# A hybrid decoder layer on one core: the first FFN block scaled between the last residual additions, the FFN zone's tags in another order, and all low parts of the first activations on VectorE

## The chip, the cores and the metric

The kernel runs on one core of one Trainium2 chip. The metric is the device time of one execution in microseconds, the median of several runs. TensorE (PE) multiplies matrices, with its weight loads (PEld) beside them; VectorE (DVE), ScalarE (ACT) and GpSimd (POOL) work element by element; SyncE (SP) holds the queue from which the transfers between HBM and the on-chip memory (SBUF) are issued, in order. Each engine runs its own instructions in a fixed order and waits on semaphores for the others. TensorE adds up in PSUM, eight banks that DVE and ACT empty.

## The reference, cut to what matters

One layer of a decoder on a prompt of 1,024 positions and 8 sequences of 8 new positions, 1,088 columns in all. Model width is 1,024, FFN width 2,816.

```
h = rms_norm(x, norm_mix_g);  proj = h @ w_in
a = silu(layer_norm(conv31(a_val * sigmoid(a_gate))))
o = attend(q, k, v)                       # three dilated windows merged
x = x + concat([a, o]) @ w_out            # residual, then:
h = rms_norm(x, norm_ffn_g)
g = conv3(concat([ffn_past, h @ w_ffn_gate]))
x = x + (silu(g) * (h @ w_ffn_up)) @ w_ffn_down
y = rms_norm(x, norm_final_g)
```

The change lies from the end of `@ w_out` to the start of `@ w_ffn_down`.

## The kernel before, in words

**Number format.** A float32 operand is split into a high part (`hi`, ACT's copy to a rounded type) and a low part (`lo = x - hi`, a subtraction on DVE or POOL). A product takes three matmuls: weights hi by x hi, hi by lo, lo by hi. Lines 908, 910, 911 (`block_product`), 926, 928, 930 (`two_products`) and 182 to 184 (`gemm`) are such triples.

**Zones.** SBUF is handed out in zones that follow each other. Zone F holds the end of the output projection and the FFN; zone D, the down projection, comes after it in the same place; zones G and U (parts of the output projection, masks and caches of the attention on new positions) and P (masks, queries, keys, values of the attention on the prompt) lie under F. A zone's tags lie one behind the other in the order in which each is first asked for, and a tile waits only for the readers of what lay in its own bytes before (`reuse_waits="tile"`). So the order of first requests sets which early reader each tile waits for. Before, F's order is b11, t2, b21, WA, t4, t1, t3, tmp, b22, sft, cfo. Most are tags of 8 slots of 544 columns (`slot`, L896); WA has 2 of 1,024 columns, tmp 4 of 544; sft and cfo hold the FFN convolution's states. Within a tag the first request takes the lowest slot, the next ones come from the top downwards. That puts t2 and the first slot of b21 on the operands of zone G, which the products of the second part of the output projection read to their end. In zone D the 24 slots of tag X (1,088 columns, the first activations' hi and lo) start at the same address as F: the first tile on F's lowest tag, the other eleven of the first group at the top of X, on t3, t1, t4 and the end of WA.

**End of the output projection (L942 to L1079).** The last two of eight input tiles are loaded in halves of 544 columns (L949), split (L951 on ACT, L952 on DVE), and so are their weights (L962, L963). `out_half(h, hook)` runs over the eight output tiles m of one half: a product of 12 matmuls, the residual addition on DVE (L1045), a store of x, the square on ACT (L1048) and its addition to a running sum on DVE (L1052). `hook` is called at the end of each m. In the second half it puts in the norm of the first half: `root` after m = 2 (10 small matmuls at L204, small DVE operations L206 to L219, a square root on ACT), `spread` after m = 5 (5 transposes L231, copies L233), which gives the scale `rb` per column.

**First blocks of the FFN (L1072 to L1136).** The FFN products work on 2 by 2 blocks in the manner of Winograd and Strassen: seven block products from seven tags b11 ... t4. `first_blocks` scales four tiles of x (`scale`, L1058 on DVE) and splits each (`split`, L972 on ACT, L973 on DVE) into b11, then b21. Its orders: the scaling waits for the last but one split, or, ahead of the first two, for `after`, the last addition of squares; each split waits for `after` too. `first_half` starts the gate's products on b11 with `two_products`. The second half's norm follows the same way.

**FFN pairs (L1175 to L1250).** Eleven pairs of tiles: gate products, convolution, up products, and `u = silu(g) * up` (L1217 is its multiplication, L1226 the additions ahead of it), which is stored to HBM. Each set of products reads the blocks in the order b11, t2, b21, t1, t3, b22, t4. `weight_blocks` makes seven weight blocks by additions on DVE and splits on ACT (L1001) and POOL (L1002).

**Down projection (L1264 to L1330).** u is read back in groups of 3 + 3, 3 + 3, 3 + 3 and 2 + 2 tiles: load (L1268, SP queue), high part on ACT (L1269), low part (L1271) on DVE, or on POOL for numbers 3 and 5 of all (`ONPOOL`). For each output tile m, weights are split (L156 on ACT, L158 on POOL), and chunks of 384, 384 and 320 columns are multiplied and added to x on DVE (L1301). x is read back from HBM by `reload`; the last two tiles of u are stored at m = 0 (L1295). PSUM has five banks for these products, so the sixth chunk needs the first to be empty. `behind(late, early)` orders two instructions of one engine; `AHEAD` puts some low parts ahead of the last pair's operations: number 1 ahead of the last addition to u, number 4 ahead of the last two multiplications.

The order of instructions on every engine is made at build time by a scheduler that runs its own model of the program; `tc.issue_after` and `behind` are orders given to it by hand.

Of the kernel before, what the change touches and what calls it, by code (L numbers as in the profile page):

```python
# [60 lines left out]
AHEAD, ONPOOL = ((1, 2), (4, 0), (4, 1)), (3, 5)  # L61
# [17 lines left out]
def trunk_kernel(tc, xT, w_in, w_out, w_gate, w_up, w_down, par, kc, vc, sa, sf, pmask, smask,  # L79
                 yT, kT, vT, ca, cas, cf):  # L80
    nc = tc.nc
    with (
# [60 lines left out]
        def behind(late, early):  # L143

            tc.add_manual_dep(late, early.name, mybir.DependencyInfo(mybir.DependencyClass.NoSync,
                                                                     mybir.DependencyReason.DATA))
# [794 lines left out]

        k0 = first[0]  # L942
        n = PARTS[-1]
        part = []
        for h, tag in enumerate(("b11", "t2")):
            part.append([])
            for i in range(n):
                raw = slot("b11", "mx", F32)
                last_load = nc.sync.dma_start(raw, mixed[k0 + i][:, h * HN:h * HN + HN]).ins  # L949
                hi, lo = slot(tag, "mh"), slot(tag, "ml")  # L950
                nc.scalar.activation(hi, raw, AF.Copy)  # L951
                nc.vector.tensor_sub(lo, raw, hi.bitcast(F32))  # L952
                part[h].append((hi, lo))
        wl = []
        for m0 in (0, 4):
# [3 lines left out]
            for i in range(2):  # L959
                r = raw[:, i * 512:i * 512 + 512]  # L960
                hi, lo = slot("b21", "wh", w=512), slot("b21", "wl", w=512)
# [35 lines left out]
        def block_tile(x, zone=False):  # L997

            t = zt("F", "WA", 2, "wa", D, F32R) if zone else wp.tile([P, D], F32R, tag="W", name=nm("wb"))
# [8 lines left out]
        def weight_blocks(w, j):  # L1008
# [6 lines left out]
            nc.vector.tensor_add(x, u1, u2)  # L1015
# [14 lines left out]
        for i in range(2):  # L1030
            up0 += weight_parts(raw[0][:, i * half:i * half + half], [slot("t4", "wa", w=half) for _ in range(2)])
# [5 lines left out]
        def out_half(h, hook):  # L1037


            c = slice(h * HN, h * HN + HN)  # L1040
            for m in range(KT):
# [3 lines left out]
                added = nc.vector.tensor_add(x, all_of(ps), x).ins  # L1045
# [3 lines left out]
                if m == 0:  # L1049
                    acc = s  # L1050
                else:
                    added = nc.vector.tensor_add(acc, s, acc).ins  # L1052
                hook(m, added)
            return acc, added
# [5 lines left out]
        def new_root(s):  # L1060
            return slot("t3", s, F32)

        sq0, _ = out_half(0, lambda *_: None)
        rs = []

        def norm_first(m, added):
            if m == 2:
                rs.append(root(sq0, D, HN))
            elif m == 5:
                rs[0] = spread(rs[0], new_root, HN)  # L1070

        def first_blocks(k, tag, after):  # L1072
            for i in range(k, k + 4):
                with tc.issue_after(made[-2] if len(made) > 1 else after):
                    scale(0, i, rs[0])
                with tc.issue_after(after):
                    split(x2[i][:, :HN], tag, i - k)

        sq1, added = out_half(1, norm_first)  # L1079
        quads = [(*halves(x2[k]), *halves(x2[k + 4])) for k in range(4)]  # L1080

        def first_half(w, between=lambda: None, hook=lambda k, last: None):
# [4 lines left out]
            shared = [zt("F", "tmp", 4, "ta", HN) for _ in o]  # L1087
# [16 lines left out]
        def between():  # L1104
            rs.append(root(sq1, D, HN))
            first_blocks(4, "b21", added)
# [6 lines left out]
        first_blocks(0, "b11", added)  # L1113
# [24 lines left out]
        sft = zt("F", "sft", 1, "sft", NF * B * 2).rearrange("p (j b t) -> p j b t", b=B, t=2)  # L1138
        nc.sync.dma_start(sft, sf)
        cfo = zt("F", "cfo", 1, "cfo", NF * 18).rearrange("p (j c) -> p j c", c=18)  # L1140
# [24 lines left out]
        stores, timed = [], {}  # L1165
# [9 lines left out]
        def ffn_pair(j):  # L1175
# [40 lines left out]
            def times(i, a, e):  # L1216
                timed[i] = nc.vector.tensor_mul(u[i][:, a:min(e, S)], u[i][:, a:min(e, S)], cv[i][:, a:min(e, S)]).ins  # L1217
# [44 lines left out]
        split_last = []  # L1262

        def load_act(j):  # L1264
# [5 lines left out]
            eng = nc.gpsimd if len(split_last) in ONPOOL else nc.vector  # L1270
            split_last.append(eng.tensor_sub(lo, raw, hi.bitcast(F32)).ins)  # L1271
# [14 lines left out]
        def down(j0, n, act, first, between):  # L1286
            for m in range(KT):
# [12 lines left out]
                def ev(ps, t0, n, x=x2[m]):  # L1300
                    nc.vector.tensor_add(x[:, t0:t0 + n], ps[:, :n], x[:, t0:t0 + n])  # L1301
# [22 lines left out]
        for k, i in AHEAD:  # L1324
            behind(timed[i], split_last[k])
# [171 lines left out]
```

## Time and profile before

| | us |
|---|---|
| runs | 1393.05, 1383.58, 1389.17; median 1389.17 |
| profiled execution | 1384.67 (span 1382.3, mean granted clock 0.991) |
| TensorE busy, matmul / weight loads | 1340.1 / 1274.5 |
| DVE, ACT, POOL busy | 832.9, 522.7, 429.3 |

The stages around the change: the second part of the output projection ends near 586 us from the span's start, its last part ends near 622, the FFN's products run to 1099, and the down projection starts there.

How to read the lines: a timeline row is start, duration, engine, source line, operation, output <- inputs, sizes, and how many instructions were merged (xN); in brackets stand the idle time of the engine before it and what ended it. A row of waits is who waited, for whom, total time, how often, the longest. A row of a group is the line, engine, operation, count, then minimum/median/maximum duration in ns. "Half clock" is a granted TensorE clock of 0.50.

### The profile page before, as it was taken

How to read it: one execution, taken by the hardware profiler on the slowest of the kernel's cores; microseconds unless marked ns; L12 is line 12 of the kernel's file. 1: busy time of each engine (PE TensorE's matmuls, PEld its weight loads, DVE VectorE, ACT ScalarE, POOL GpSimd, SP SyncE). 2: the span in 40 equal slices, each digit the busy share in tenths (PEclk: the TensorE clock that was granted, in tenths of full speed). 3: DMA queues.
4: the chain of work that ended last, by engine and by line, in shares of the span. 5: the costliest groups of instructions: out<-in, count | busy, mean ns of one | idle time of the engine just before them, and what ended most of it. 6: DMA issues, size and time to landing. Idle time of an engine off the chain costs nothing.

```text
span 1382.3 us, 25035 instructions
## 1 busy us (share of the span) xinstructions
PE 1340.1 (97%) x10059; PEld 1274.5 (92%) x10059; DVE 832.9 (60%) x1660; ACT 522.7 (38%) x1047; POOL 429.3 (31%) x341
## 2 busy tenths in 40 slices
PE   7999999999999999998999999999999999999996
PEld 7998888989978877888999999999999989999996
DVE  6478878566585566578865655665656661313156
ACT  6322221457575465255533333333333430202122
POOL 1221112111010103430865554555644332223200
PEclk9999999999999999989999999999999999999998
DMA  8247675746688976460111222202212481314103
GB/s 281 68 152 274 234 264 183 204 132 154 210 269 247 268 215 229 135 206 16 64 57 68 95 79 79 94 32 95 94 64 94 140 303 54 136 46 144 40 18 113
DMA packets 85747, 195.16 MB, mean 141 GB/s; under 512 B 12672, under 2 KB 47744, under 8 KB 85632
## 3 DMA queue, kind: packets, MB, share of 16 engines
q1 hardware_dynamic: 85632, 193.57, 43.6%
q8 instruction: 79, 1.29, 0.4%
q14 instruction: 36, 0.29, 0.1%
HBM read 145.03 MB, written 48.52 MB: 140 GB/s over the span
## 4 chain that ended last, share of the span: by engine, by line
PE 88%; DMA 6%; DVE 4%; issue 1%; ACT 1%; SPq 0%; POOL 0%; DVEq 0%; ACTq 0%; POOLq 0%
PE g L182 12%; PE g L184 12%; PE g L183 12%; PE py L910 4%; PE py L908 4%; PE py L911 4%; PE o L734 3%; PE pz L910 3%; PE pz L911 3%; PE pz L908 3%; PE px L910 3%; PE px L911 3%; PE px L908 3%; PE s L649 3%; PE t L717 2%; PE ss L568 1%
## 5 line engine op out<-in xcount | busy, mean ns | idle before, releaser
L158 POOL TENSOR_TENSOR wl<-wr,wh 128x768 fp32r<-128x768 f32 (+2 forms) x60 | 114.5, 1910 | 484.9 <-PE g L184 390.7
L182 PE MATMUL g<-xh,wh 128*128 128x384 f32 (+1 forms) x472 | 158.1, 335 | 0.6 <-DVE qkv L445 0.6
L183 PE MATMUL g<-xl,wh 128*128 128x384 f32 (+1 forms) x472 | 156.9, 332 | 0.0
L184 PE MATMUL g<-xh,wl 128*128 128x384 f32 (+1 forms) x472 | 156.7, 332 | 0.0
L182 PE MATMUL g<-ah,wh 128*128 128x384 f32 (+1 forms) x432 | 140.1, 328 | 3.0 <-DVE x L1301 3.0
L184 PE MATMUL g<-ah,wl 128*128 128x384 f32 (+1 forms) x432 | 140.9, 327 | 1.7 <-POOL wl L158 1.7
L183 PE MATMUL g<-al,wh 128*128 128x384 f32 (+1 forms) x432 | 141.4, 328 | 0.4 <-POOL al L1271 0.3
L1002 POOL TENSOR_TENSOR wb<-wr,wb 128x512 fp32r<-128x512 f32 x84 | 115.6, 1388 | 56.5 <-ACT wb L1001 56.5
L156 ACT ACTIVATE wh<-wr 128x768 fp32r<-128x768 f32 (+2 forms) x60 | 50.0, 833 | 218.9 <-PE g L184 170.9
L1001 ACT ACTIVATE wb<-wr 128x512 fp32r<-128x512 f32 x84 | 52.6, 629 | 163.7 <-DVE wr L1017 104.0
L1301 DVE TENSOR_TENSOR x<-g,x 128x384 f32<-128x384 f32 (+1 forms) x72 | 37.9, 533 | 123.3 <-PE g L184 123.3
L690 ACT ACTIVATE y<-y,m 128x128 f32<-128x128 f32 (+1 forms) x192 | 88.9, 466 | 19.6 <-DVE m L678 19.5
L182 PEld LDWEIGHTS g<-xh,wh 128*128 128x128 f32 x472 | 89.2, 189 | 2.9 <-issue 1.6
L184 PEld LDWEIGHTS g<-xh,wl 128*128 128x128 f32 x472 | 89.2, 189 | 2.3 <-issue 2.1
L1207 DVE SCALAR_TENSOR_TENSOR fc<-gb,prm,fc 128x1104 f32<-128x1104 f32 x44 | 81.8, 1877 | 14.8 <-ACT fc L1205 14.5
L183 PEld LDWEIGHTS g<-xl,wh 128*128 128x128 f32 x472 | 89.4, 189 | 0.6 <-issue 0.2
L653 DVE CUSTOM_DVE_ANT_0 y<-s,pmk 128x128 f32<-128x128 f32 (+1 forms) x192 | 64.1, 379 | 41.7 <-PE s L649 31.9
L1002 POOL TENSOR_TENSOR wa<-wr,wa 128x512 fp32r<-128x512 f32 x42 | 56.0, 1336 | 100.9 <-ACT wa L1001 100.9
L395 DVE SCALAR_TENSOR_TENSOR cacc<-gp,prm,cacc 128x1024 f32<-128x1024 f32 x60 | 86.7, 1444 | 0.0
L182 PEld LDWEIGHTS g<-ah,wh 128*128 128x128 f32 x432 | 81.0, 188 | 3.8 <-DVE x L1301 3.5
L184 PEld LDWEIGHTS g<-ah,wl 128*128 128x128 f32 x432 | 81.1, 188 | 2.0 <-POOL wl L158 2.0
L183 PEld LDWEIGHTS g<-al,wh 128*128 128x128 f32 x432 | 81.2, 188 | 1.0 <-POOL al L1271 0.6
(359 smaller groups left out, 4091.0 us busy)
## 6 DMA issues: line engine op xcount, KB each, us to landing
cr<-in_kc SPq DMA_DIRECT2D x24, 768.0 KB, 6.8
cr<-in_vc SPq DMA_DIRECT2D x24, 768.0 KB, 7.4
kk<-dk SPq DMA_DIRECT2D x48, 256.0 KB, 5.9
u<-u SPq DMA_DIRECT2D x22, 544.0 KB, 4.7
al<-u SPq DMA_DIRECT2D x22, 544.0 KB, 5.1
wr<-in_w_gate SPq DMA_DIRECT2D x22, 512.0 KB, 3.4
wr<-in_w_up SPq DMA_DIRECT2D x22, 512.0 KB, 4.6
wr<-in_w_in SPq DMA_DIRECT2D x20, 512.0 KB, 5.5
```

What stands on the lines that cost most here:

```text
L158: lo_eng.tensor_sub(lo, raw, hi.bitcast(F32))
L182: nc.tensor.matmul(ps[c], whi[:, k, :], xh[:, t0:t0 + n], start=(k == 0), stop=False)
L183: nc.tensor.matmul(ps[c], whi[:, k, :], xl[:, t0:t0 + n], start=False, stop=False)
L184: nc.tensor.matmul(ps[c], wlo[:, k, :], xh[:, t0:t0 + n], start=False, stop=(k == nk - 1))
L395: eng.scalar_tensor_tensor(acc[:, :S], gp[:, j:j + S], col(w0 + j), acc[:, :S], op0=ALU.mult, op1=ALU.add)
L653: nc.vector.tensor_tensor_reduce(out=y[:, o:o + n], in0=ps[:, o:o + n], in1=mask, op0=ALU.add, op1=ALU.min, scale=1.0, scalar=3e38, accum_ ...
L690: nc.scalar.activation(y, y, AF.Exp, bias=m[:, 4 * g + i:4 * g + i + 1], scale=-1.0, accum_out=den[:, g, 2 * hd + u, i:i + 1])
L908: nc.tensor.matmul(ps, whi[:, k, :], xh[:, t], start=(start and k == 0), stop=False, skip_group_check=True)
L910: nc.tensor.matmul(ps, whi[:, k, :], xl[:, t], start=False, stop=False, skip_group_check=True)
L911: nc.tensor.matmul(ps, wlo[:, k, :], xh[:, t], start=False, stop=(k == nk - 1), skip_group_check=True)
L1002: nc.gpsimd.tensor_sub(lo, x, hi.bitcast(F32))
L1207: nc.vector.scalar_tensor_tensor(c[:, :W], gb[i][:, t:t + W], col(C_FW + 3 * f + t), c[:, :W], op0=ALU.mult, op1=ALU.add)
```

## The change

It does four things.

1. `norm_first` is called for the root after m = 3 and for the spread after m = 6, one product later each.
2. `first_blocks` gives up `after`: the first two scalings wait for the residual additions of products 6 and 7 of the second half, no longer for the last addition of squares, and the splits wait for nothing by hand. `out_half` returns its residual additions. The first addition of `weight_blocks` is put behind the last split of b21 (`made[7]`).
3. The tags of zone F are asked for in another order, by a block of early requests: cfo, sft, WA, tmp, t4, t3, b21, t2, b11, then t1, b22. The tiles asked for early are handed to the places that used to ask for them.
4. All low parts of u are made on DVE. Numbers 0 to 3 go ahead of the last addition to u, number 5 ahead of the last two multiplications, and the first two additions to x of m = 0 go ahead of these multiplications too.

```
-AHEAD, ONPOOL = ((1, 2), (4, 0), (4, 1)), (3, 5)
+AHEAD = ((3, (1, 0)), (5, 0), (5, 1))
...
+        cfo = zt("F", "cfo", 1, "cfo", NF * 18).rearrange("p (j c) -> p j c", c=18)
+        sft = zt("F", "sft", 1, "sft", NF * B * 2).rearrange("p (j b t) -> p j b t", b=B, t=2)
+        early = {"gate": [zt("F", "WA", 2, "wa", D, F32R) for _ in range(2)],
+                 "shared": [zt("F", "tmp", 4, "ta", HN) for _ in range(2)],
+                 "up": [slot("t4", "wa", w=D // 2) for _ in range(4)], "rb": [slot("t3", "rb", F32)],
+                 "b21": [slot("b21", "wh", w=512)], "t2": [slot("t2", "mh")], "b11": []}
...
-                hi, lo = slot(tag, "mh"), slot(tag, "ml")
+                hi, lo = early[tag].pop() if early[tag] else slot(tag, "mh"), slot(tag, "ml")
...
             x = zt("F", "tmp", 4, "s1", HN)[:, :half]
-            nc.vector.tensor_add(x, u1, u2)
+            with tc.issue_after(made[7]):
+                nc.vector.tensor_add(x, u1, u2)
...
-        def norm_first(m, added):
-            if m == 2:
+        def norm_first(m):
+            if m == 3:
                 rs.append(root(sq0, D, HN))
-            elif m == 5:
+            elif m == 6:
                 rs[0] = spread(rs[0], new_root, HN)
 
-        def first_blocks(k, tag, after):
+        def first_blocks(k, tag):
             for i in range(k, k + 4):
-                with tc.issue_after(made[-2] if len(made) > 1 else after):
+                with tc.issue_after(made[-2] if len(made) > 1 else residuals[6 + i]):
                     scale(0, i, rs[0])
-                with tc.issue_after(after):
-                    split(x2[i][:, :HN], tag, i - k)
+                split(x2[i][:, :HN], tag, i - k)
...
-                timed[2] = nc.vector.tensor_add(o, all_of(ps), o if x is None else x).ins
+                late[i, h] = nc.vector.tensor_add(o, all_of(ps), o if x is None else x).ins
...
-            eng = nc.gpsimd if len(split_last) in ONPOOL else nc.vector
-            split_last.append(eng.tensor_sub(lo, raw, hi.bitcast(F32)).ins)
+            lows.append(nc.vector.tensor_sub(lo, raw, hi.bitcast(F32)).ins)
...
                 def ev(ps, t0, n, x=x2[m]):
-                    nc.vector.tensor_add(x[:, t0:t0 + n], ps[:, :n], x[:, t0:t0 + n])
+                    added = nc.vector.tensor_add(x[:, t0:t0 + n], ps[:, :n], x[:, t0:t0 + n]).ins
+                    if first and m == 0 and t0 < S // 2:
+                        behind(late[1 if t0 else 0], added)
...
-        for k, i in AHEAD:
-            behind(timed[i], split_last[k])
+        for k, to in AHEAD:
+            behind(late[to], lows[k])
```

More of the change, by code (lines that the diff above doesn't have):

```diff
@@ L141, in trunk_kernel, with behind @@
         weights_read = [None]
[L143 to L146 removed]
+        def behind(later, earlier):
+            tc.add_manual_dep(later, earlier.name, mybir.DependencyInfo(mybir.DependencyClass.NoSync,
+                                                                        mybir.DependencyReason.DATA))
         def load_w(src, nk, lo_eng, new=None):
@@ L1105, in between @@
             rs.append(root(sq1, D, HN))
-            first_blocks(4, "b21", added)
+            first_blocks(4, "b21")
         def spread_second(k, last):
@@ L1164, in trunk_kernel @@
         ud = [dp.tile([P, N], F32, name=f"u{j}") for j in range(NF)]
-        stores, timed = [], {}
+        stores, late = [], {}
         M = S - HN
```

34 lines of the change are left out of this document (18 added, 16 removed).

## The prediction

> **What bounds the kernel now.** I read the page first, then busy time by stage, TensorE's own waits, and last the timeline around each wait.
>
> ```profile
> PE 1340.1 (97%) x10059; PEld 1274.5 (92%) x10059; DVE 832.9 (60%) x1660; ACT 522.7 (38%) x1047; POOL 429.3 (31%) x341
> ```
> ```profile
> 586.00:626.00 40.00, 31.99 (x214) 30.87 (x212) 32.29 (x49) 21.38 (x38) 12.48 (x8) 0.87 0.56 191
> 626.00:680.00 54.00, 53.91 (x417) 53.45 (x418) 50.31 (x77) 31.22 (x51) 23.98 (x14) 0.97 0.00 1
> 680.00:800.00 120.00, 120.00 (x958) 120.00 (x957) 73.72 (x91) 42.84 (x61) 65.82 (x67) 1.00 0.25 82
> 1090.00:1130.00 40.00, 36.69 (x234) 35.27 (x234) 21.78 (x22) 12.52 (x13) 14.05 (x6) 1.00 0.86 309
> ```
>
> The windows' columns are length, then busy time with count of PE, PEld, DVE, ACT and POOL, granted clock, DMA share, GB/s. TensorE is the bound. Inside the FFN (680 to 800) it never idles, so nothing there can be won. The change touches two stages where TensorE does idle: 586 to 626 (40.0 - 32.0 = 8.0 us idle, clock 0.87) and 1090 to 1130 (3.3 us idle, full clock). TensorE's waits name them:
>
> ```profile
> PE px L926 <- DVE x L1058: 3.7, 1, 3.7
> PE g L182 <- DVE x L1301: 3.0, 2, 2.4
> PE g L204 <- DVE sq L1052: 2.1, 1, 2.1
> ```
>
> The idle time is not the whole price. TensorE alone, in windows cut where its clock changes (busy, count, granted clock):
>
> ```profile
> 589.04:592.45 3.41, 3.18 (x14) 0.50 0.80 252
> 592.45:606.10 13.65, 13.65 (x111) 1.00 0.67 233
> 609.50:612.90 3.40, 3.40 (x18) 0.50 0.84 261
> 612.90:616.30 3.40, 3.40 (x17) 0.50 0.62 229
> 626.60:630.00 3.40, 3.40 (x17) 0.50 0.00 0
> ```
>
> At full clock a matmul of this stage takes 13.65/111 = 0.123 us, so a product of 12 takes 1.48. Every wait is followed by half clock: 14 matmuls take 3.18 us where 14 x 0.123 = 1.7 would do. The three stretches cost 3.18 - 1.7 = 1.5; for 609.5 to 616.3, less 1.2 us of the root's small matmuls, 5.6 us for 25 matmuls, 5.6 - 3.1 = 2.5; and 3.4 - 2.1 = 1.3.
>
> **Part A: the zone's layout, at its start.** No instruction is added; tags only move. Before, the first weight slot (b21) and the t2 slots lie on tiles that the previous stage's products still read.
>
> ```profile
> 579.93 1.37 SPq L949 DMA_DIRECT2D mx<-mixed  x3
> 585.40 1.67 ACT L962 ACTIVATE wh<-wr 128x512 fp32r<-128x512 f32 x3 [12.33 <-PE g L184]
> 586.29 0.49 DVE L857 TENSOR_TENSOR x<-g,x 128x320 f32<-128x320 f32 x1 [0.76 <-PE g L184]
> 587.68 0.77 PE L908 MATMUL g<-mh,wh 128*128 128x272 f32 x4 [1.43 <-ACT mh L951]
> 589.27 0.60 PE L910 MATMUL g<-ml,wh 128*128 128x272 f32 x1 [0.82 <-DVE ml L952]
> ```
> ```profile
> mx<-mixed SPq DMA_DIRECT2D x4, 272.0 KB, 4.7
> ```
>
> ScalarE stood 12.33 us for that one slot, with mh queued behind wh on it; hence TensorE's 1.43 and 0.82. After, b21 lies on the caches' buffers, and t2 and b11 on the query, key and mask tiles, all read for the last time before 575 by the stage order. Then the input's landing sets the halves: last issue by 581.3, + 4.7 = 586.0, about when the previous products end (587.68 - 1.43 = 586.25). Something remains: the first accumulator lies on banks that the last addition empties at 586.29 + 0.49 = 586.8, so 0.5 of the 1.43 stays. Gain 0.9 + 0.8 + 1.5 of half clock = 3.2. Bounds: 0 (the input lands later) and 3.8 (no wait). I take 3.2, since the input's row gives 586.0. The weight loads behind come earlier too, with POOL's low parts of them; eight are made there before and after, so DVE meets as many.
>
> **Part B: root after product 3 instead of 2, spread after 6 instead of 5.** The root issues 10 matmuls, DVE's small operations and a square root on ScalarE; the spread 5 transposes and 2 copies. None is added.
>
> ```profile
> 593.51 0.73 DVE L1045 TENSOR_TENSOR x<-g,x 128x544 f32<-128x544 f32 x1 [3.05 <-PE g L911]
> 608.24 0.71 DVE L1052 TENSOR_TENSOR sq<-sq,sq 128x544 f32<-128x544 f32 x1
> 609.10 1.64 PE L204 MATMUL g<-ones,sq 128*128 128x1 f32 x10 [2.10 <-DVE sq L1052]
> 614.82 0.17 DVE L219 SCALAR_TENSOR_TENSOR rr<-rt,rr 128x5 f32<-128x5 f32 x1
> 617.82 0.77 PE L231 MATMUL g<-ident,rr 128*128 128x128 f32 x5
> 618.46 0.69 ACT L233 ACTIVATE rb<-g 128x512 f32<-128x512 f32 x2 [0.47 <-PE g L231]
> ```
>
> DVE needs 593.5 to 608.95 = 15.4 us from the first residual addition to the last square. After part A the first product starts at 586.8 and is added at about 588.6, so the squares end at 604.0. Twelve products end at 586.8 + 12 x 1.48 = 604.6: the 2.10 go, and with them the cause of 2.5 us at half clock. What is late next is the spread: root to rr took 614.99 - 609.10 = 5.9 us, the cover is the root and three products, 1.6 + 4.4 = 6.0. Nothing is spare, so I give 0.8, about half a product, back: gain 3.8. Bounds: -0.8 (the 2.1 come back at the spread with the 0.8 on top, and half clock stays) and 4.6. [...]
>
> **Part C: two scalings between the residual additions.**
>
> ```profile
> 621.50 0.28 PE L911 MATMUL g<-mh,wl 128*128 128x272 f32 x1
> 621.82 0.72 DVE L1045 TENSOR_TENSOR x<-g,x 128x544 f32<-128x544 f32 x1 [0.74 <-PE g L911]
> 622.47 1.54 DVE L1052 TENSOR_TENSOR sq<-sq,sq 128x544 f32<-128x544 f32 x2
> 623.92 1.48 DVE L1058 SCALAR_TENSOR_TENSOR x<-x,prm,rb 128x544 f32<-128x544 f32 x2
> 625.43 0.72 DVE L973 TENSOR_TENSOR b11l<-x,b11h 128x544 fp32r<-128x544 f32 x1
> 625.45 0.40 PE L926 MATMUL px<-b11h,wa 128*128 128x272 f32 x1 [3.66 <-DVE x L1058]
> 626.91 0.59 PE L928 MATMUL px<-b11l,wa 128*128 128x272 f32 x1
> ```
>
> Call T the end of the residual products (621.8 before). DVE runs the last residual addition, two squares, two scalings, the low part, and TensorE gets on at 626.91 = T + 5.1. After, the first scaling waits for the spread (0.70), its copy (0.69) and itself (0.74): 2.1 us after product 6, when product 7 ends (0.70 + 1.48 = 2.2). So it is done at T; DVE's last residual addition is the work queued behind its wait and is not held up. The high part follows at T + 0.7. The low part comes after residual 7, scaling 1 and perhaps a square: 0.65 + 0.74 + 0.65 + 0.72 = T + 2.4 to 2.8; with 1.1 us of the second root still to run that is 3.5 in place of 5.1, 1.6 gained. Of the 1.3 at half clock I take half, 0.7, as the slack stretch shrinks but stays. Gain 2.3; bounds 0.7 (one scaling) and 4.9 (the whole 3.66 and 1.3). DVE is busy 50.31 of the next 54 us: its 3.7 spare exceed 2.3, so the gain isn't eaten there. The addition of `weight_blocks` that now waits for the last b21 split is not needed by then.
>
> **Part D: into the down projection.** The new layout puts the first six activation tiles on b11, t2 and b21, which the last FFN products read first, instead of t3, t1 and t4, read last. Two low parts go from POOL to DVE.
>
> ```profile
> SPq L1268 <- PE pz L911: 12.1, 2, 11.7
> SPq L1295 <- DVE u L1217: 7.0, 2, 6.0
> ```
> ```profile
> L1271 DVE TENSOR_TENSOR al<-al,ah x20: 1276/1293/2996, 1097.5 to 1257.1; 128x1088 fp32r<-128x1088 f32 x20
> ```
> ```profile
> 1105.11 0.45 PE L183 MATMUL g<-al,wh 128*128 128x384 f32 x1 [0.28 <-POOL al L1271]
> 1106.13 5.77 DVE L1217 TENSOR_TENSOR u<-u,fc 128x480 f32<-128x480 f32 x2
> 1111.82 1.41 DVE L1301 TENSOR_TENSOR x<-g,x 128x384 f32<-128x384 f32 x3
> 1112.41 0.42 PE L182 MATMUL g<-ah,wh 128*128 128x320 f32 x1 [2.36 <-DVE x L1301]
> 1127.94 0.42 PE L182 MATMUL g<-ah,wh 128*128 128x320 f32 x1 [0.59 <-DVE x L1301]
> ```
>
> The loads waited 12.1 us in the queue for t1 and t3. The products run in the order b11, t2, b21, t1, t3, b22, t4, so that the last of the three is read out after three of seven. Earlier loads let DVE make all six low parts (6 x 1.29 = 7.7 us) before 1105; the first two x additions then go ahead of the multiplications, which took 5.77. Removed: 0.28 + 2.36 + 0.59 = 3.2. The added order makes the multiplications later, and the two stores of u (L1295) behind them, and behind those on SP the later reloads; but SP waited 7.0 there already and the cover, eight products of a whole group, is long. The final u addition after four low parts frees no bank that comes soon. I take 2.6, 0.6 back for the later stores. Bounds: -10.2 (six low parts at the longest 3.0 instead of 1.29) and 3.2.
>
> **Sum.** 3.2 + 3.8 + 2.3 + 2.6 = 11.9 us. The profiled execution took 1384.67, so it would take 1372.8; it is 4.5 below the median 1389.17 but inside the runs (1383.58 to 1393.05), and I set the gain against the median: 1377.3.
>
> **Rivals.**
> - Everything closes and the clock never falls: 3.2 + 4.6 + 4.9 + 3.2 = 15.9, 1373.3. For it: at full clock 592.45 to 606.10 shows no idle. Against: the low part still has to follow a residual addition.
> - The waits only move, since DVE is the one that TensorE awaits in B and C: A's 3.2, one scaling 0.7 and D's 2.6 remain, 6.5, 1382.7. For it: 32.29 of 40 us busy, and nothing spare ahead of the spread.
> - Half clock does not come from waits as short as A's and B's and stays: 11.9 - 1.5 - 2.5 = 7.9, 1381.3. For it: it began after 1.43 + 0.82 of idle, not more. Against: each of the stretches follows an idle one. [...]
> - Slower, at the start of the down projection: DVE's low parts are held up by POOL's weight parts. At 3.0 each six need 18.0 us where some 8 (1094 to 1102) are covered: TensorE stands 10, loses 2.6 more at half clock, and D's 2.6 don't come: 9.3 - 12.6 = -3.3, 1392.5. It turns at an average of about 2.4 us (8 + 9.3 - 2.6 over six). Against: median 1.29. [...]
>
> **Chances.** Forecast 0.50, all closes 0.17, waits move 0.20, clock stays 0.08, slower 0.05. A measurement tells about 1% (13.9 us) from no change. Faster by more, under 1375.3: the second case and 0.08 of the first, 0.25. Slower by more: 0.02 of the last. Range 1369 to 1388: from the all-closing case with 4 us for the base (the profiled run's distance from the median) to the moved waits with 5; outside are most of the slower case and the edges, under 0.2.
>
> **What would show it.** A: no TensorE wait over 0.6 at the zone's start, the first ACT wh before 585. B: L204 without a DVE wait, no half clock behind it. C: L928 within 4 us of the last L911. D: no SP wait of L1268 on pz, no L1301 wait over 0.5. Wrong if L231 waits, if half clock follows no idle time, or if L1271 runs near 3 us.

## The result, and the profile after

The changed kernel takes 1381.12 us (median of 20 runs, 1374.04 to 1387.83), the kernel before 1387.88 (20 runs, 1381.44 to 1393.05), run in turn on one chip: a ratio of 0.9948, 95% interval 0.9931 to 0.9964, so 5.0 to 9.6 us faster. The forecast was a gain of 11.9 us; the time lies in the forecast's range. The gain is under the 1% that the prediction took for the least that a measurement tells from no change, but this interval is narrower and does not reach 1. The profiled execution took 1379.77 us, span 1377.8, 4.9 less than the one before.

Lines of the changed kernel stand 8 to 13 lower in the file: L959 and L960 are the input's high and low parts, L970 and L971 the weights', L1058 the residual addition, L1065 the addition of squares, L1071 the scaling, L980 and L981 the blocks' parts, L1278 to L1280 the load of u and its parts, L1227 the multiplication for u, L1310 the addition to x.

Busy time by stage, TensorE alone (length, busy, count, granted clock, DMA share, GB/s), first the kernel before, then the changed one. The cuts are the end of the second part of the output projection, the first product on b21, and the start of the down projection:

```profile
0.00:586.25 586.25, 567.57 (x4386) 1.00 0.66 207
586.25:634.41 48.16, 40.06 (x266) 0.86 0.46 159
1099.36:1382.30 282.94, 267.50 (x1709) 0.99 0.33 111
```
```profile
0.00:592.89 592.89, 573.15 (x4386) 0.99 0.65 205
592.89:634.08 41.19, 35.75 (x266) 0.96 0.54 186
634.08:1099.02 464.94, 464.42 (x3702) 1.00 0.23 77
1099.02:1377.80 278.78, 267.33 (x1709) 0.98 0.32 107
```

From the first cut on, this pair of profiles shows 48.16 - 41.19 = 7.0 and 282.94 - 278.78 = 4.2 us gained, 11.1 in all, almost the forecast; and 592.89 - 586.25 = 6.6 us lost ahead of it, where nothing was changed: every engine's order is the same there. The 6.6 us are the clock's: ahead of that cut the trace of the kernel before has one stretch of half clock (3.41 us), that of the changed kernel four. Over the twelve profiles with the same orders up to there it is one to six, and the cut lies some 2.2 us later with each (correlation 0.93). So neither number is the effect of the change: two profiles of one stage differ by what the clock did in them, and the experiments had to separate that from the rest.

TensorE's waits from the first cut on, up to the tail (who waited, for whom, sum, times, longest), and SP's around the start of the down projection:

```profile
PE g L910 <- DVE ml L960: 1.6, 1, 1.6
PE px L928 <- DVE b11l L981: 1.4, 1, 1.4
PE px L926 <- ACT b11h L980: 1.1, 1, 1.1
PE g L183 <- DVE al L1280: 0.8, 2, 0.4
PE g L908 <- DVE x L857: 0.7, 1, 0.7
PE g L204 <- DVE sq L1065: 0.6, 1, 0.6
PE pz L908 <- ACT wb L1012: 0.5, 1, 0.5
```
```profile
SPq L1278 <- PE px L911: 4.1, 1, 4.1
SPq L1304 <- DVE u L1227: 4.0, 2, 3.3
```

The root's wait went from 2.1 to 0.6, the wait ahead of the first block from 3.7 to two of 1.1 and 1.4, those on x at the down projection from 3.0 to none. The last row is a new wait inside the FFN, for the high part of a weight block. It goes with the order that puts the additions of `weight_blocks` behind the last split of b21: of the nine kernels with that order all but e4 (below) show it, of the five without it none; the prediction held that addition for not needed by then. At the zone's start 1.43 + 0.82 became 0.7 + 1.6: nothing. The timeline there shows why:

```profile
584.59 1.15 ACT L970 ACTIVATE wh<-wr 128x512 fp32r<-128x512 f32 x2 [4.88 <-DMA mixed<-cat]
592.93 0.49 DVE L857 TENSOR_TENSOR x<-g,x 128x320 f32<-128x320 f32 x1 [0.76 <-PE g L184]
593.34 1.88 DVE L971 TENSOR_TENSOR wl<-wr,wh 128x512 fp32r<-128x512 f32 x3
595.14 0.72 DVE L960 TENSOR_TENSOR ml<-mx,mh 128x544 fp32r<-128x544 f32 x1
593.57 0.74 PE L908 MATMUL g<-mh,wh 128*128 128x272 f32 x4 [0.68 <-DVE x L857]
595.91 0.40 PE L910 MATMUL g<-ml,wh 128*128 128x272 f32 x1 [1.61 <-DVE ml L960]
```

ScalarE was freed: its high parts begin 8.3 us before the zone. But in DVE's order three weight low parts stand behind the last addition and ahead of the first input's low part, so L910 waits until 595.9.

At the first block, the rows that answer to part C:

```profile
622.08 0.78 DVE L1071 SCALAR_TENSOR_TENSOR x<-x,prm,rb 128x544 f32<-128x544 f32 x1
622.22 0.29 PE L911 MATMUL g<-mh,wl 128*128 128x272 f32 x1
624.05 0.77 DVE L1071 SCALAR_TENSOR_TENSOR x<-x,prm,rb 128x544 f32<-128x544 f32 x1
624.74 0.72 DVE L981 TENSOR_TENSOR b11l<-x,b11h 128x544 fp32r<-128x544 f32 x1
625.51 0.59 PE L928 MATMUL px<-b11l,wa 128*128 128x272 f32 x1 [1.40 <-DVE b11l L981]
```

The first scaling is made while the last residual product runs; the low part still stands behind the second scaling.

### The profile page after: what moved, and what is told of

It is laid out like the page before. It is cut to its first block, busy times and chain, and to the rows that moved or that the text cites. A ratio compares the mean times of both kernels' runs of the same rounds, so it can differ in the third digit from the quotient of the medians.

```text
span 1377.8 us, 25042 instructions
## 1 busy us (share of the span) xinstructions
PE 1340.6 (97%) x10059; PEld 1274.3 (92%) x10059; DVE 829.7 (60%) x1662; ACT 521.2 (38%) x1047; POOL 419.6 (30%) x339
## 4 chain that ended last, share of the span: by engine, by line
PE 84%; DVE 7%; DMA 5%; issue 1%; ACT 1%; SPq 1%; DVEq 0%; ACTq 0%
PE g L184 11%; PE g L182 11%; PE g L183 11%; PE py L910 4%; PE py L908 4%; PE py L911 4%; PE o L734 3%; PE pz L908 3%; PE px L908 3%; PE pz L910 3%; PE px L911 3%; PE pz L911 3%; PE px L910 3%; PE s L649 3%; PE t L717 2%; DVE cacc L395 2%
## 5 line engine op out<-in xcount | busy, mean ns | idle before, releaser
L156 ACT ACTIVATE wh<-wr 128x768 fp32r<-128x768 f32 (+2 forms) x60 | 49.9, 832 | 223.6 <-PE g L184 187.5
L1310 DVE TENSOR_TENSOR x<-g,x 128x384 f32<-128x384 f32 (+1 forms) x72 | 38.1, 533 | 126.9 <-PE g L184 126.9
L1013 POOL TENSOR_TENSOR wa<-wr,wa 128x512 fp32r<-128x512 f32 x42 | 62.1, 1482 | 143.5 <-ACT wa L1012 127.8
L1217 DVE SCALAR_TENSOR_TENSOR fc<-gb,prm,fc 128x1104 f32<-128x1104 f32 x44 | 82.4, 1891 | 14.8 <-ACT fc L1215 14.4
```

The lines of the kernel that those rows point to most:

```text
L1013: nc.gpsimd.tensor_sub(lo, x, hi.bitcast(F32))
L1217: nc.vector.scalar_tensor_tensor(c[:, :W], gb[i][:, t:t + W], col(C_FW + 3 * f + t), c[:, :W], op0=ALU.mult, op1=ALU.add)
```

## The experiments

Ratios are to the kernel before, measured beside each (95% interval). A stage's length is that from the first cut to the second block, 48.16 and 41.19 above.

**e1 to e3: the parts by themselves.** e1 is the kernel before with the block of early requests; e3 with only these lines of the down projection:

```
-AHEAD, ONPOOL = ((1, 2), (4, 0), (4, 1)), (3, 5)
+AHEAD = ((3, (1, 0)), (5, 0), (5, 1))
...
+            lows.append(nc.vector.tensor_sub(lo, raw, hi.bitcast(F32)).ins)
...
+                    if first and m == 0 and t0 < S // 2:
+                        behind(late[1 if t0 else 0], added)
```

e2 has only points 1 and 2 of the change, the root, the spread and the scalings; its main lines:

```
-            if m == 2:
+            if m == 3:
...
-            elif m == 5:
+            elif m == 6:
...
-                with tc.issue_after(made[-2] if len(made) > 1 else after):
+                with tc.issue_after(made[-2] if len(made) > 1 else residuals[6 + i]):
```

> The kernel before with the new order of zone F's tags alone. Theory 1 (from the two traces: the wait at the zone's start only went from ScalarE to DVE): ScalarE's 12.33 us wait is gone, but TensorE still idles 2.0 to 2.5 us at the start of the zone, 1.2 to 1.8 of it on a DVE low part; the waits of SP for pz at the down projection go, TensorE's there stay near 3; 0 to 3 us below the kernel before. Rival (the prediction's part A and half of D): no wait over 0.6 at the zone's start, and 4 to 6 us below.

> The kernel before with the later root and spread and the two scalings between the residual additions, old order of tags. Theory 1: the root's 2.10 us wait shrinks to under 1 (the squares still end late, since the zone starts as before), L928 comes 3.0 to 3.5 us after the last L911 in place of 5.1; without half clock 3 to 4 us below, and up to 3.4 more where stretches of half clock go, so 3 to 6 below the kernel before. Rival (the waits only move): under 2 us below, with a wait of the spread's transposes (L231) over 1.

> The kernel before with all low parts of u on DVE, four of them and two additions to x ahead in DVE's order, old order of tags. Theory 1: the loads still wait some 12 us on SP for tags t1 and t3, so the low parts come late and the additions to u, queued behind four of them, with them; the L1301 waits of 2.36 and 0.59 go but a wait on a low part of 0.5 to 3 takes their place: within 2 us of the kernel before. Rival (the orders alone do the work, the layout nothing): 2.4 to 3.2 below, TensorE's waits there under 1 in sum.

Measured: e1 1.0011 (0.9989 to 1.0032), e2 0.9969 (0.9950 to 0.9987), e3 1.0023 (1.0003 to 1.0044). The layout alone gains nothing, and e1 shows the same 0.7 and 1.6 us at the zone's start as the changed kernel. At the down projection SP's loads no longer wait on pz, as expected, but a wait on a low part took the place of those on x (its L1281 is the low part of u; DVE, POOL, TensorE):

```profile
1110.29 4.81 DVE L1281 TENSOR_TENSOR al<-al,ah 128x1088 fp32r<-128x1088 f32 x2
1110.62 3.33 POOL L1281 TENSOR_TENSOR al<-al,ah 128x1088 fp32r<-128x1088 f32 x1 [4.13 <-ACT ah L1279]
1115.15 0.44 PE L183 MATMUL g<-al,wh 128*128 128x384 f32 x1 [2.14 <-DVE al L1281]
```

The loads now come early enough for DVE's and POOL's low parts to fall together; DVE's take 2.4 us each there, and TensorE waits 2.14, with half clock behind it (from 1116.86 us its matmuls on 320 columns start 0.27 us apart, in place of 0.15 from 1132.60). With all on DVE, in the changed kernel, four take 1.23 each:

```profile
1097.16 4.90 DVE L1280 TENSOR_TENSOR al<-al,ah 128x1088 fp32r<-128x1088 f32 x4
1107.44 0.56 DVE L1310 TENSOR_TENSOR x<-g,x 128x384 f32<-128x384 f32 x1 [1.05 <-PE g L184]
```

The multiplications for u, ahead of the additions to x in the kernel before, show the same. There a low part on POOL starts just ahead of them, and they take 5.77 us (the L1217 row in the prediction's part D); in the changed kernel POOL has no low part, and they take 0.65 and 1.22 (first POOL before, then DVE after):

```profile
1105.78 2.83 POOL L1271 TENSOR_TENSOR al<-al,ah 128x1088 fp32r<-128x1088 f32 x1 [0.72 <-ACT ah L1269]
```
```profile
1107.91 0.65 DVE L1227 TENSOR_TENSOR u<-u,fc 128x480 f32<-128x480 f32 x1
1108.94 1.22 DVE L1227 TENSOR_TENSOR u<-u,fc 128x1024 f32<-128x1024 f32 x1
```

In e5 and e6 (below) POOL's low part is first too: they take 5.76, and TensorE waits 2.4 on x. In e2 they start 0.4 us ahead of POOL's low part and take 4.12, and TensorE's waits there sum to 0.5 in place of 3.3, without the new layout and without the new orders. No run moves the low parts off POOL by itself, so how much of D's gain is that and how much the orders stays open.

e3, the orders without the layout, is slower, if barely; its trace shows a longer chain (SP's waits; then ACT, DVE and TensorE; L156 is a weight's high part, L1276 and L1277 the parts of u, L1307 the addition to x):

```profile
SPq L1286 <- DMA u<-u: 4.9, 2, 2.7
```
```profile
1126.90 0.85 ACT L156 ACTIVATE wh<-wr 128x768 fp32r<-128x768 f32 x1 [6.84 <-DMA wr<-in_w_down]
1129.34 1.29 DVE L1277 TENSOR_TENSOR al<-al,ah 128x1088 fp32r<-128x1088 f32 x1 [7.95 <-ACT ah L1276]
1131.16 0.63 PE L182 MATMUL g<-ah,wh 128*128 128x320 f32 x1 [2.63 <-DVE x L1307]
```

The first store of u there is issued 11.2 us behind the start of the down projection in place of 9.8; a reload of x (L1286) waits in SP's queue for a store of u; a weight load behind it lands late; ScalarE makes the next group's high part late; and the additions to x stand behind that low part on DVE, with a bank that TensorE wants. This chain is read from the trace; no run tried a link of it by itself.

**e5 and e6: root and scalings apart.** e5 is e2 without the scalings, e6 is e2 with the root at m = 2 and the spread at m = 5. **e7** is the layout and the down projection without either, that is, e1 and e3 together.

> The kernel before with the root after product 3 and the spread after product 6, nothing else. Theory 1: the 2.10 us wait of the root's matmuls shrinks to about 0.6 and the spread does not wait, the 3.7 us wait ahead of L926 stays: 1.5 us of idle and, in the runs where that wait had brought half clock behind it, up to 3.4 more, on the mean 2 to 4 us below the kernel before. Rival (the prediction's low end): the wait comes back at L231, within 1 us of the kernel before.

> The kernel before with the two scalings between the residual additions, root and spread where they were. Theory 1: L204's 2.10 us wait and the half clock behind it stay, the 3.7 us ahead of the first block becomes two waits of 2.5 in sum: 1 to 2.5 us below the kernel before. Rival (C is the larger part of the gain of both): 3 us or more below.

> The kernel before with the order of tags and the start of the down projection, root and scalings as before. Theory 1 (each needs the other: the layout alone changed nothing, the orders alone cost 3 us): TensorE's waits at the start of the down projection fall to about 1 us, no half clock there, 2 to 4 us below the kernel before. Rival (the parts add up): layout +1.5 and orders +3.3 by their own runs, so 2 to 5 us above the kernel before.

Measured: e5 0.9965 (0.9939 to 0.9990), e6 0.9992 (0.9967 to 1.0017), e7 0.9971 (0.9946 to 0.9995). The later root gains by itself; the scalings alone can't be told from no change, although their wait falls from 3.7 to 0.7 + 1.5 us. The two intervals overlap, so the times don't say which is worth more. TensorE's idle time in the stage is 8.1 us before (48.16 - 40.06), 7.1 in e5, where the wait ahead of the first block grows to 4.1, 6.7 in e6, and 5.4 in e2 as in the changed kernel: of the idle time each takes its share. What sets e5 apart is the clock (below). e7 gains 4 us (0.0029 x 1387) where its halves gave +1.5 and +3.2: they need each other. With e2's 4.3 that makes 8.3, next to the 6.8 measured for the whole; some of e2's 4.3 may come from the down projection, by its shorter waits there.

**e4 and e8: mending the zone's start and the first block.** Both are the changed kernel with orders on DVE. In e4 the low parts move ahead into the gaps between the last additions of the part before (`ends`); in e8 they stay behind the last addition but in the order of need, and the first block's low part goes ahead of a scaling and an addition of squares:

```
+        behind(ends[-3], low[4])
+        behind(ends[-1], low[0])
+        behind(low[6], low[1])
```
```
+        behind(low[4], low[0])
+        behind(low[5], low[1])
...
+        behind(sums[5], made[0])
+        behind(scaled_x[1], made[0])
+        behind(scaled_x[2], made[1])
```

(`low`: the inputs' low parts 0 to 3, the weights' 4 to 7.)

> The changed kernel with three low parts at the zone's start ordered ahead: the first weights' low part ahead of the first addition of the last output tile of the part before, the first input's ahead of its last addition, the second input's ahead of the third weights'. Theory 1: the 1.61 us wait on a DVE low part goes, the 0.7 on the bank stays, no half clock follows there: 1.6 us below the changed kernel, up to 3.3 where a stretch of half clock goes with it. Rival: the input lands too late, the last addition waits for it and the first product with it: 0 to 2 us above the changed kernel.

> The changed kernel with two orders added: the low parts of the first two inputs ahead of those of the first two weights at the zone's start, and the first block's low part ahead of the second scaling and the addition of squares that stood before it. Theory 1: the 1.61 us wait at the zone's start goes (0.7 on the bank stays), L928 comes 2.0 us after the last L911 in place of 3.0, and with no idle of 2 us in one place fewer stretches of half clock: 2 to 4 us below the changed kernel, 9 to 11 below the kernel before. Rival (DVE is full there: the second scaling or the second norm is late instead): a wait of L926 or L928 of the second tile, or of L231, over 1, and no more than 1 us below the changed kernel.

Measured: e4 0.9934 (0.9911 to 0.9958), e8 0.9945 (0.9923 to 0.9967). In e8 the 1.6 us at the start went, and L926 and L928 wait 0.9 instead of 2.5, as expected. What came instead stands in its waits around the first blocks:

```profile
PE g L204 <- DVE sq L1071: 2.7, 2, 2.3
PE g L908 <- DVE x L857: 0.7, 1, 0.7
PE px L926 <- ACT b11h L983: 0.5, 1, 0.5
PE px L928 <- DVE b11l L984: 0.4, 1, 0.4
```

The root waits 2.3 us again: 0.7 + 2.3 in place of 2.3 + 0.6. TensorE's earlier start doesn't make DVE's eight low parts, eight residual additions and seven additions of squares any shorter, and the root stands at their end. A's wait and B's wait are one slack. e4 takes work out of that stretch, into gaps where DVE was idle; there TensorE waits 0.7 ahead of the zone, 1.2 at its start and 0.3 at the root. A stretch of half clock still follows at the start of its zone (from 590.33 us a matmul every 0.23 us in place of 0.12), which its expectation had excluded.

**e11: four low parts on POOL.** e8 with the third and fourth weights' and the second half's inputs' low parts on POOL, which idles there for 15.66 us in the changed kernel:

```
-                low.append(nc.vector.tensor_sub(lo, raw, hi.bitcast(F32)).ins)
+                low.append((nc.gpsimd if h else nc.vector).tensor_sub(lo, raw, hi.bitcast(F32)).ins)
...
-                low.append(nc.vector.tensor_sub(lo, r, hi.bitcast(F32)).ins)
+                low.append((nc.gpsimd if m0 else nc.vector).tensor_sub(lo, r, hi.bitcast(F32)).ins)
```

> The kernel of e8 with four of the eight low parts at the zone's start on POOL: those of the third and fourth weights and of the second half's two inputs. Theory 1 (DVE's work between the zone's start and the root is one budget, so what A saves comes back as B's wait: 2.3 + 0.6 us in the changed kernel, 0.7 + 2.3 in e8): with 2.5 us taken off DVE there the start waits 0.7 and L204 under 0.6, from the end of the part before to the second block 36.5 to 39.5 us in place of 41.2, 3 to 5 us below the changed kernel and 9 to 12 below the kernel before. Rival (POOL's low parts slow DVE beside them, or the wait goes on to L231 or L926): 40 us or more there, within 1.5 us of the changed kernel.

Measured: 0.9954 (0.9936 to 0.9973), the stage 43.2 us: theory 1 fell, and the rival's 40 us or more came. The timeline (L1015 is the gate weights' high part, L1071 the addition of squares, L1064 the residual addition):

```profile
594.50 3.47 POOL L971 TENSOR_TENSOR wl<-wr,wh 128x512 fp32r<-128x512 f32 x2 [8.95 <-ACT wh L970]
602.91 1.15 ACT L1015 ACTIVATE wa<-wr 128x512 fp32r<-128x512 f32 x2 [3.05 <-DMA wr<-in_w_gate]
604.64 0.84 DVE L1071 TENSOR_TENSOR sq<-sq,sq 128x544 f32<-128x544 f32 x1 [3.46 <-ACT sq L1067]
611.24 1.64 DVE L1071 TENSOR_TENSOR sq<-sq,sq 128x544 f32<-128x544 f32 x1
612.81 0.71 DVE L1064 TENSOR_TENSOR x<-g,x 128x544 f32<-128x544 f32 x1
611.00 3.02 POOL L1004 TENSOR_TENSOR wa<-wr,wa 128x512 fp32r<-128x512 f32 x2 [0.90 <-ACT wa L1003]
```

ScalarE waits 3.05 us for the gate weights' load; the squares are queued behind that copy, and DVE stands 3.46 us without them. The likely cause is the weight buffer, which POOL reads until 597.97; that link was argued from the order and not tried by itself.

**e12 and e14: the clock.** e12 is the changed kernel with 19 stalls in the FFN, run once (1516.3 us); its extra matmuls write a column that the next product overwrites. e14 is the changed kernel once more.

```
+            for _ in range(1 + 2 * (count[0] % 6)):
+                nc.scalar.activation(t, t, AF.Copy)
...
+            return nc.tensor.matmul(x[:, PO:PO + 1], t, ones, start=True, stop=True, skip_group_check=True).ins
```

> The changed kernel with 19 stalls of TensorE put into the FFN, where it does not idle: ahead of a pair's first product a one-column matmul waits for a chain of 2, 4, 6, 8, 10 or 12 small copies on ScalarE that starts when the product before ends. Theory 1 (the clock is set by fixed windows of 3.41 us: about 2 us of idle within one window brings half clock in the next): every stretch of half clock there begins on one grid of 3.41 us, each follows a window with 1.7 us or more of idle, no window with less than 1.6 is followed by one, and stalls of 2 to 3 us are followed or not by where the grid cuts them. Rival 1 (a stall's length alone decides): all stalls above one length are followed, wherever they lie. Rival 2 (half clock comes by chance, or from load): no order, or as many stretches behind short stalls as behind long ones.

> The changed kernel once more, beside e11 on the same chip, with a second profile. Theory 1 (order and code ahead of the output projection's end are those of the kernel before; the scatter of the whole time comes from there and from the clock): that end lies anywhere between 586 and 600 us, the stage from there to the second block again takes 39.5 to 43 us, and the time is 4 to 9 us below the kernel before. Rival (the change makes the part ahead of it longer): that end is again 4 us or more behind the mean of the kernels with the old order of tags (590.9).

e14 measured 0.9967 (0.9949 to 0.9984), with its first cut at 593.41 and a stage of 42.99 us. It has the very waits of the first profile at the zone's start, 0.7 and 1.6, and another clock. TensorE in windows laid on the clock's grid, the changed kernel's first profile and then e14 (length, busy, count, clock):

```profile
594.33:597.74 3.41, 1.83 (x14) 1.00 0.48 159
597.74:601.15 3.41, 3.41 (x29) 1.00 0.65 230
```
```profile
593.64:597.05 3.41, 1.36 (x9) 1.00 0.23 65
597.05:600.46 3.41, 3.41 (x18) 0.50 0.71 245
```

The grid cut 1.58 us of idle into one window in the first (3.41 - 1.83), 2.05 into one in the second, and only the second lost the clock: 18 matmuls in 3.41 us in place of 29. e12 shows it with stalls (one that half clock followed and one that it didn't, each with the window behind it):

```profile
722.94:726.35 3.41, 1.20 (x10) 1.00 0.65 192
726.35:729.76 3.41, 3.41 (x17) 0.50 0.82 225
...
1064.26:1067.67 3.41, 1.79 (x15) 1.00 0.33 129
1067.67:1071.09 3.42, 2.83 (x23) 1.00 0.84 226
```

The stalls came out longer than meant (92.1 us in 19 waits, 4.8 each), so few lie near the limit. All that theory 1 named came out. In e12 alone a limit on a stall's length would fit as well: the shortest one followed by half clock took 2.49 us, from the matmul before it to the next product, the longest one not followed 2.46. Against it stand the pair above, the same waits with and without half clock, and two stalls of 9.3 us, in which the clock fell one window apart, as the grid cut 2.11 us off the one and 1.89 off the other. So in these runs a window's share of the idle decided, not a wait's length.

**e15: a faster kernel.** e4's three orders and e8's three for the first block.

> The kernel of e4 with e8's order at the first block (its low part ahead of the second scaling and of an addition of squares). Theory 1 (e4's low parts ran in DVE's gaps ahead of the zone, so they leave no later work to the root, unlike e8's; the first block's low part then saves what it saved in e8): TensorE's waits from the zone's start to the second block 3.5 us or less in sum in place of 5.4 in the changed kernel, L204 under 0.6, L926 and L928 1.0 in sum; from the end of the part before to the second block 36 to 39 us with one stretch of half clock in it, 2 to 4 us below the changed kernel, 8 to 11 below the kernel before. Rival (as in e8 the squares come late and the root waits 1.5 or more, the rest is the clock's draw): within 1.5 us of the changed kernel, and e4's lower time was a draw too.

Measured: 0.9917 (0.9886 to 0.9948), 7.2 to 15.8 us under the kernel before; the changed kernel's two measurements are 0.9948 and 0.9967. TensorE's waits from the zone's start into the second block sum to 3.0 us (1.2, 0.9, 0.4, 0.3, 0.2; 0.7 more lie ahead of the zone) in place of 5.4, and the stage has no half clock at all:

```profile
590.80:628.26 37.46, 34.45 (x266) 1.00 0.60 205
```

It beats the kernel before; against the changed kernel, which wasn't timed beside it, its interval overlaps that of the first measurement and ends just under that of the second, and how much of the distance is the clock's luck can't be said from seven runs.

## Why the prediction was right or wrong

**The number.** 11.9 us were forecast, 6.8 measured (5.0 to 9.6), and 4.6 (2.2 to 7.1) beside e14. The range held it. Part A makes most of the distance, the price put on half clock may make the rest. By the time alone two rivals lie nearer than the forecast, half clock stays (1381.3) and the waits only move (1382.7), but neither is what the traces show: TensorE's idle time in the stage fell from 8.1 to 5.4 us, and the half clock behind the root went.

**A (3.2 forecast).** Wrong. By e1 the layout alone gives -4.4 to +1.5 us, counted as a gain, around -1.5; TensorE's idle time in the stage is 8.1 us with it (e1, e7) and without it. The step that failed is "the input's landing sets the halves": it followed ScalarE and the transfer and left out DVE, which had three weight low parts (1.88 us) to make behind its last addition before the one that was awaited. The 0.5 on the bank was right (0.68). The 12.33 us that ScalarE stood were real and worth nothing by themselves.

**B (3.8).** Right: e5 gives 4.9 (1.4 to 8.5), and the mechanism, a wait that brings half clock with it, held. The wait fell from 2.10 to 0.58 (0.60 in e5) and the spread waited for nothing, so the 0.8 given back for it was not needed. Of e5's gain 1.0 us is idle time in its trace (1.3 forecast, 2.1 - 0.8), and its runs lose 3.8 us less to the clock than the kernel before beside them (2.5 forecast). With an interval this wide, that the sum comes so near is in part luck. The premise, that the zone's start comes earlier and the squares with it, was wrong; the root's later place alone did it.

**C (2.3).** The mechanism was right, the size can't be confirmed: L928 comes 625.51 - 622.22 = 3.3 us behind the start of the last L911 in place of 626.91 - 621.50 = 5.4, and e6 has 1.4 us less idle (1.6 forecast), but its time gives 1.1 (-2.4 to 4.6). The new wait of 0.5 us in the FFN was put at nothing. B and C together, e2, give 4.3 (1.8 to 6.9) for 6.1 forecast.

**D (2.6).** Right in size, and right that it takes more than one of its parts: e7 gives 4.0 (0.7 to 7.5), of which A has no part by e1. From the start of the down projection to the end the four profiles that have none of D take 279.0 to 282.9 us (before, e2, e5, e6; mean 281.1), the eight that have all of it 278.0 to 279.4 (mean 278.8). The 279.0 is e2's. TensorE's 3.2 us there (0.28 + 2.36 + 0.59) became 0.8. The later stores of u, priced at 0.6, are by its trace where e3's longer chain starts when the loads aren't early. The "slower" rival's mechanism exists, but in e1: DVE's low parts at 2.4 us beside POOL's. With POOL's two moved over it is gone (e7); and the 5.77 us of the multiplications, which the prediction took as given, stood beside a low part on POOL too (0.65 and 1.22 without one).

**The clock.** 4.7 of the 11.9 were half-clock stretches that stood in one profile, taken as a fixed price, and "every wait is followed by half clock" was too much: the 2.36 us at the down projection stand at full clock, with 1.24 and 1.12 us of idle in the two windows that they fall into. The changed kernel's code shows none of them between the two cuts in e12 (39.91 us), one in its own profile (41.19) and two in e14 (42.99), with the same waits each time: each costs about 1.5 us.

So two of the three places were a draw: half clock stands behind the zone's start in four of the fourteen profiles (before, e4, e5, e14), at the first block in eleven, for one window to three. The root's was none. Counted as idle, as the windows below ask for, its ten one-column matmuls (1.2 to 1.9 us) and a wait of 2.1 to 2.3 us ahead of them make over 3 us together: half clock follows in all six profiles with such a wait (before, e1, e3, e6, e7, and e8, where it came back), and in none of the eight whose root waits 1.5 us or less.

The times agree. What the clock costs, span times (1 - mean granted clock), is on the mean 16.2 to 17.3 us for the kernel before (four sets, 96 runs), 16.1 to 18.5 for the others with the old root (e1, e3, e6, e7), and 11.4 to 15.1 for all with the later one (12.6 for e5; 13.6 and 15.1 for the changed kernel, 20 and 12 runs). So 1 to 3 us of the gain are clock, not 4.7, and it comes with the root.

What the prediction lacked is the grid. In the fourteen profiles the first change to full clock lies 8.0 to 11.4 us behind the start (8.8 in the kernel before, 10.7 in the changed one), and all later changes lie whole windows of 3.413 us from it; idle time of 1.66 to 1.90 us in one window was enough for half clock in the next. A price by the wait alone leaves out where the borders cut it and what lies beside it: the root's wait was 2.10 us, but with the one-column matmuls (1.64) idle time of 3.7 us lies there.

**The base.** The gain was rightly set against the median and not the profiled time: over the twelve profiles with the same orders up to the first cut, that cut lies between 586.25 (the kernel before, the earliest of all) and 599.87 us (e1). That the new layout itself delays it, e14's rival, has little for it: e14's cut at 593.41 is 2.5 us behind the 590.9 of the old layout's mean, not 4, and the means of the two layouts over all fourteen profiles, 593.2 and 590.9, differ about as their stretches of half clock ahead of it do (3.2 and 2.4 a profile).

**What would show it.** Of the signs named, the first high part ahead of 585 us, no half clock behind the root, L231 without a wait, L928 within 4 us, no SP wait of L1278 on pz and no L1310 wait came true. The zone's start did not (1.6 us in place of 0.6 at most), and L204 still waits 0.6 us on DVE.

## What to carry to other kernels

Follow every input of the awaited instruction back to its own engine's queue, and look up what stands ahead of it in that order: a wait that ends last hides the others, and here a free ScalarE only showed a busy DVE. Two waits fed by one full engine are one slack; to gain, move its work into a gap ahead of the stretch (e4, e15); moving it along the stretch (e8) or to POOL (e11) gained nothing here. A half-clock stretch seen in one profile may be a draw or may come every time: add up the wait and the one-column matmuls beside it, ask whether they fill more than 1.90 us of a 3.41 us window wherever its borders fall (with more than that half clock always followed here, with less than 1.66 never), and compare stages over several profiles. And a length read from one row, like the 5.77 us (0.65 and 1.22 with no low part on POOL), may be that of a neighbour's work: look up what POOL does beside it.

## What the runs showed of the hardware

**The clock by windows.** Over all 14 profiles, from 583 us on and without the last two windows of each, in windows of the grid that the clock's own changes lie on (3.413 us), and with the one-column matmuls counted as idle: of 3208 windows at full clock 54 were followed by half clock. None of them had under 1.66 us of idle, no window above 1.90 went without, and of the eleven between these four were followed and seven not. At half clock, 66 windows ahead of the last stretch of each profile, the clock stayed down where the idle was 0.80 us or more and came back where it was 0.67 or less. So in these profiles half clock always followed a window under 44% busy (1.90 us idle) and never one over 51% (1.66), and full clock came back behind windows 80% busy or more (0.67). The one-column matmuls have to count as idle for this: counted as busy, windows with no idle time at all would keep half clock, as at 609.53 us in the kernel before (3.42 of 3.42 us busy with them, 1.13 idle without). Both limits were found in the windows that they describe; only e12's were foretold (1.6 to 1.7 us).

**The scatter is mostly this clock.** Among the 20 runs of the changed kernel the fastest, 1374.04 us, had a mean granted clock of 0.994 and the slowest, 1387.83, 0.985; span times (1 - clock) is 8.2 and 20.8, 12.6 of the 13.8 us between them, and over the 20 runs it correlates with the time at 0.88.

**DVE beside POOL.** In e11 the addition of squares, both of whose inputs lie in SBUF, took 1.64 us beside POOL's weight parts (611.00 to 614.02), in place of 0.71 with POOL idle in the kernel before (606.97), and the residual addition, which has one input in PSUM, 0.71 right behind it, beside the same parts. The rows of the kernel before agree: its sixteen residual additions took 0.71 to 0.73 us, with POOL beside them or not; of its fourteen additions of squares the six with POOL idle took 0.71 to 0.73, seven beside POOL 1.16 to 1.82, and one that began 0.16 us ahead of POOL's part 0.71 (608.24). That it is where the inputs lie that matters was not tried by itself.
